# Single-head scores in the even block, transposed retention queries and keys, and a new order of the first loads in a three-block fp32 transformer kernel

## The chip, the cores and the metric

The kernel runs on one core of a Trainium2 chip. The metric is the device time in microseconds (us) from launch to end. The engines are TensorE (PE, matrix products; PEld are its weight loads), VectorE (DVE), ScalarE (ACT), GpSimd (POOL) and SyncE (SP, which here only issues DMA transfers).

## The reference

Batch 1, 256 tokens, width 1024, everything in fp32. Three blocks follow one another, and a last rmsnorm ends the program.

```
# block 0 (even): two kinds of attention, then an MLP
h = rmsnorm(x, g);  qa, ka, va, qb, kb, vb = split(h @ w_in_e)
qa, ka, qb, kb = rmsnorm per head of 64
oa = window attention: 8 query heads over 2 kv heads, ALiBi slopes, a sink per head
ob = neighbourhood attention: 8 heads, relative position bias
x = x + concat(oa, ob) @ w_out_e;  x = x + relu(rmsnorm(x) @ w1)**2 @ w2
# block 1 (odd): retention, then an MLP
q, k, v, g = split(rmsnorm(x) @ w_in_o)      # 8 heads, dk = 128, dv = 256
y = forward retention + backward retention (decays per head)
x = x + (silu(g) * groupnorm(y)) @ w_out_o;  x = x + MLP(x)
# block 2: moba + indexed sparse + cross attention, gated and merged
z = rmsnorm(x) @ w_in;  u = sum of three gated branches;  x = x + u @ w_out
return rmsnorm(x, g_final)
```

## The kernel before

All weights stream from memory in chunks of 1 MB (the first two in quarters) into four `raw` buffers, in the order in which they are used: `load` and `w_dma` issue them on SP's queue, each chunk when its buffer is free. ACT copies a chunk to `whi` in a rounded format (fp32r), DVE makes the rest `wlo = raw - whi`, half a chunk at a time. Activations are split in the same way (`xh`, `xl`). Each product is three matmuls, high by high, high by low and low by high (`mm3`), so a name such as `whi,xh` in a row is moving operand, stationary operand. `panel` computes 512 columns of a product for the 256 tokens with x as the stationary operand and the weights moving: 8 blocks of the width by 2 token tiles by 3, 48 matmuls of 512 columns (one of 256 columns wide takes 48 of 256). `panel_T` holds the weights and moves x, 256 tokens at a time, so its result lies transposed, features by tokens; for the same 512 columns it takes 96 matmuls of 256 columns.

Fp32 matmuls without a split are the attention scores (`kTa,qTa` for the window heads, `kTb,qTb` for the neighbourhood heads) and the PE transposes (`const,qn`, `const,p`, `const,nat`, `const,at`). A score is a product over 64 features. The heads of a pair lie in rows 0 to 63 and 64 to 127 of the array, and `score_pair` writes their matmuls alternately, for each of two token tiles one matmul of each head, into two banks. `even_head` follows for each head: a DVE pass adds the bias table and finds the maximum, ACT takes the exponential, DVE normalises, PE transposes p (`const,p`), ACT and DVE split it (`ph`, `pl`), and PE multiplies by v.

A scheduler inside the build writes one order for each engine. Tasks are generators. Each operation asks for an engine, has a cost in a table and becomes ready when its inputs are (by the same costs); of the ready operations the one with the lowest priority number goes first. `MEM`, `BIAS` and `DMA0` are times in the scheduler's own clock from which mem, the bias tables and the first transfers count, and `pads()` and `distances()` are low-priority tasks that start at a time of that clock. The order that comes out is fixed in the program; on the chip each engine follows it and waits where an input is late.

Start-up: `warm()` fills PE with bf16 matmuls of zeros until the third half-chunk of weights is split. The first panel (qa) runs from chunks 0 and 1, the second (ka with va, 256 columns, here called the ka panel) from chunks 2 and 3, and then qb, kb and vb. In the odd block, for each of four pairs of heads (hp), a `panel` computes q and k of both heads, ACT copies the result to `nat`, PE transposes it in two groups of four, and ACT and DVE split it into `qk`; then come a panel for v and one for the gate.

Of the kernel before, what the change touches and what calls it, by code (L numbers as in the profile page):

```python
# [72 lines left out]
class Kernel:  # L73
# [17 lines left out]
    MEM, BIAS = 14.0, 16.0  # L91

    DMA0, FINE = 1.5, 4
# [299 lines left out]
    def load(self, eng, out, in_):  # L393

        eng.dma_start(out, in_)
        n = out.shape[0] * self._n(out) * 4
        self.free["D"] += max(n / 360e3, 0.18)
        self._mark(self.ready, out, self.free["D"] + 1.7, "D")

    def w_dma(self, a=None, b=4):  # L400
# [13 lines left out]
        else:  # L414
            self.nc.sync.dma_start(raw[:, :n], src)
            t0 = max(self.free["D"], self.rawfree[i - self.RAW] if i >= self.RAW else 0.0)
            self.free["D"] = t0 + P * n * 4 / 360e3
# [259 lines left out]
    def split_T(self, src, hi, lo, k0, t, key, scale=None):  # L677
# [8 lines left out]
        if k0 is None:  # L686
            pv = ps[:, :n * P].rearrange("p (a b q) -> p a b q", a=2, b=n // 2)
        else:
            pv = ps[:, :n * P].rearrange("p (i q) -> p i q", i=n)
            hi, lo = (v[:, k0:k0 + n, t * P:(t + 1) * P] for v in (hi, lo))  # L690
# [46 lines left out]
    def even_head(self, pool, ps, v, o, j, tab, init, sink=None):  # L737


# [102 lines left out]
    def run(self):  # L842
# [24 lines left out]
        self.w_dma(0, 4)  # L867
        for t in range(NT):
            self.load(nc.sync, x[t], aps["x"][t * P:(t + 1) * P, :])
        self.load(nc.sync, const, aps["const"][:, :K_MAIN])  # L870
        for _ in range(self.RAW - 2):
            self.w_dma()
# [9 lines left out]
    def warm(self):  # L882
# [6 lines left out]
        yield 1.4  # L889
        while self.hcur < 3:  # L890
# [4 lines left out]
            self._pe(0.213 if self.now < 7 else 0.11, ps)  # L895
# [36 lines left out]
    def _even(self, pool):  # L932
# [62 lines left out]
        self.spawn(pads(), 12.0, self.LOW)  # L995
# [16 lines left out]
        self.spawn(distances(), 20.0, self.LOW)  # L1012
# [15 lines left out]
        def even_heads():  # L1028

            self.res["hd"] = self.hb  # L1030
            for j in range(0, 16, 2):
# [4 lines left out]
                if j % 4 == 0:  # L1036
# [3 lines left out]
                qT, kT = (qTa, kTa[:, 0, :]) if j < 8 else (qTb, kTb[:, j // 2 - 4, :])  # L1040
                rows = [slice(0, 64), slice(64, P)]
                ps = yield from self.score_pair([[(t * S, (t + 1) * S, qT[r, j // 2 % 4, t * P:(t + 1) * P], kT[r])
                                                  for r in rows] for t in range(NT)])
                self.fire(("s", j), ("s", j + 1))
                for i in range(2):
                    yield ("acq", "hd", 1)
                    self.spawn(head_a(j + i, o, ps[i]) if j < 8 else head_b(j + i - 8, o, ps[i]))
# [34 lines left out]
        def head_a(j, o, ps):  # L1082
            h, n = A_ORDER[j], j % 2
            vc = slice(64 * n, 64 * n + P)
# [4 lines left out]
            return self.even_head(pool, ps, lambda kt: (va[kt][0][:, vc], va[kt][1][:, vc]), o, j, tab,  # L1089
# [7 lines left out]
        def head_b(h, o, ps):  # L1097
# [4 lines left out]
            return self.even_head(pool, ps, lambda kt: (vb[kt][0][:, vc], vb[kt][1][:, vc]), o, 8 + h, tab, 3e38)  # L1102
# [127 lines left out]
    def _odd(self, pool):  # L1230
# [32 lines left out]
        def qk_task(hp, qk):  # L1263
            def task(t, ps):
                yield ("acq", "nat", 1)
                nat = pool.tile([P, 512], F32, name="nat", tag="nat", bufs=2)
                yield from self.act(nat, ps, AF.Copy)
                self.done(ps)
                yield from self.split_T(nat, *(vap(v[:, t * P:], [[KO, 2], [S, 2], [1, P]]) for v in qk), None, t,
                                        ("rqk", hp, t))  # L1270
                self.give("nat")
            return task
# [100 lines left out]
        for hp in range(4):  # L1373
# [5 lines left out]
            yield from self.panel(self.xT, "xo", qk_task(hp, qk), tmajor=hp == 0)  # L1379
            for hh in range(2):  # L1380
                self.spawn(head(hp, hh, qk, vv, sg), hh * 4.0)
            yield from self.panel(self.xT, "xo", v_task(hp, vv))
# [375 lines left out]
def _layout(inputs):  # L1758
# [32 lines left out]
    for hp in range(4):  # L1791
        parts += [w[:, hp * 256:(hp + 1) * 256], w[:, D + hp * 256:D + (hp + 1) * 256],
                  w[:, 2 * D + hp * 512:2 * D + (hp + 1) * 512], w[:, 4 * D + hp * 512:4 * D + (hp + 1) * 512]]
# [38 lines left out]
```

## Time and profile before

| what | value |
| --- | --- |
| median of 3 runs | 996.02 us (996.0, 996.02 and 997.14) |
| profiled execution | 997.11 us, its span 995.3 us |
| PE busy | 982.2 us, 99% of the span |
| DVE, ACT, POOL busy | 675.1, 525.9 and 30.4 us |
| granted clock, mean | 0.997 of full speed |
| DMA | 175.71 MB, 177 GB/s on average |

The span runs from the first to the last instruction of the profile; 1.8 us of the execution lie outside it. Busy time of PE is time with at least one matmul under way. Because matmuls are pipelined, a matmul's own duration is longer than the step from one start to the next, and the step is what a matmul costs in a stream.

### The profile page before, as it was taken

The page shows a single profiled execution, that of the slowest core. Times are in us where ns is not written, and L with a number is a line of the kernel's source. Part 1 is how long each engine was busy: PE and PEld are TensorE (multiplying, and loading weights), DVE is VectorE, ACT ScalarE, POOL GpSimd, SP SyncE. Part 2 cuts the span into 40 slices and gives each one's busy share as a digit, 9 for nine tenths or more (in the row PEclk, how much of TensorE's full clock was granted, in tenths as well). Part 3 has the DMA queues.
Part 4 walks back from the last instruction along what each step waited for, and adds up shares of the span by engine and source line. Part 5 has one row for each costly group of instructions (what it writes and reads, how often), then busy time and mean ns, then how long its engine had stood idle before and what let it go on. Part 6 is the DMA issues. An engine that isn't in the chain of part 4 may idle for free.

```text
span 995.3 us, 14096 instructions
## 1 busy us (share of the span) xinstructions
PE 982.2 (99%) x5559; PEld 844.6 (85%) x5559; DVE 675.1 (68%) x1134; ACT 525.9 (53%) x821; POOL 30.4 (3%) x38
## 2 busy tenths in 40 slices
PE   8999999999999999999999999999999999999997
PEld 6787889999998888888889999998888888878885
DVE  6898567554457977877657555446779866677774
ACT  7777656433345655555446553334564554454453
POOL 1220000000000000000000000000100000000000
PEclk9999999999999999999999999999999999999999
DMA  9733455555445544443555555542544436544431
GB/s 351 285 133 122 134 175 205 218 209 202 170 169 175 184 166 163 167 168 138 194 187 171 209 209 214 212 171 97 203 157 141 156 139 205 192 173 148 180 127 42
DMA packets 27266, 175.71 MB, mean 177 GB/s; under 512 B 3200, under 2 KB 3584, under 8 KB 7616
## 3 DMA queue, kind: packets, MB, share of 16 engines
q1 hardware_dynamic: 25776, 171.49, 48.0%
q0 software_dynamic: 704, 2.49, 1.0%
q8 instruction: 43, 0.70, 0.3%
q10 hardware_dynamic: 720, 0.84, 0.3%
q14 instruction: 23, 0.19, 0.1%
HBM read 173.75 MB, written 1.05 MB: 176 GB/s over the span
## 4 chain that ended last, share of the span: by engine, by line
PE 97%; DVE 2%; ACT 0%; DMA 0%; issue 0%; POOL 0%; DVEq 0%; POOLq 0%
PE bank L332 93%; PE bank L343 4%; DVE p L279 1%; DMA tb<-in_xT 0%; DVE pl L257 0%; DVE p L265 0%; DVE st L289 0%; PE bank L894 0%; ACT ph L252 0%; ACT nraw L252 0%; ACT u L252 0%; DVE x L257 0%; DVE wlo L257 0%; ACT qn L252 0%; DVE o L257 0%
## 5 line engine op out<-in xcount | busy, mean ns | idle before, releaser
L257 DVE TENSOR_TENSOR wlo<-raw,whi 128x1024 fp32r<-128x1024 f32 (+2 forms) x266 | 311.5, 1183 | 89.6 <-ACT whi L252 87.9
L252 ACT ACTIVATE whi<-raw 128x1024 fp32r<-128x1024 f32 (+2 forms) x266 | 268.5, 1024 | 131.9 <-PE bank L332 131.3
L332 PE MATMUL bank<-whi,xh 128*128 128x512 f32 (+2 forms) x592 | 233.8, 397 | 2.2 <-ACT whi L252 2.2
L332 PE MATMUL bank<-wlo,xh 128*128 128x512 f32 (+2 forms) x592 | 227.5, 384 | 0.4 <-DVE wlo L257 0.4
L332 PE MATMUL bank<-whi,xl 128*128 128x512 f32 (+2 forms) x592 | 227.7, 385 | 0.0
L332 PEld LDWEIGHTS bank<-whi,xh 128*128 128x128 f32 x592 | 112.2, 190 | 23.0 <-ACT whi L252 3.1
L332 PEld LDWEIGHTS bank<-whi,xl 128*128 128x128 f32 x592 | 112.2, 190 | 22.2
L332 PEld LDWEIGHTS bank<-wlo,xh 128*128 128x128 f32 x592 | 112.5, 190 | 19.7 <-DVE wlo L257 0.6
L332 PE MATMUL bank<-xh,mlo 128*128 128x256 f32 x464 | 128.2, 276 | 0.0
L332 PE MATMUL bank<-xh,mhi 128*128 128x256 f32 x464 | 128.2, 276 | 0.0
L332 PE MATMUL bank<-xl,mhi 128*128 128x256 f32 x464 | 128.2, 276 | 0.0
L257 DVE TENSOR_TENSOR h<-h 128x512 f32<-128x512 f32 x32 | 22.0, 688 | 115.4 <-ACT h L252 115.4
L332 PE MATMUL bank<-whi,hh 128*128 128x512 f32 x256 | 100.2, 391 | 0.0
L332 PE MATMUL bank<-wlo,hh 128*128 128x512 f32 x256 | 99.8, 390 | 0.0
L332 PE MATMUL bank<-whi,hl 128*128 128x512 f32 x256 | 99.7, 389 | 0.0
L252 ACT ACTIVATE h<-bank 128x512 f32<-128x512 f32 x32 | 18.8, 588 | 137.4 <-PE bank L332 137.4
L332 PEld LDWEIGHTS bank<-xh,mhi 128*128 128x128 f32 x464 | 87.1, 188 | 0.5
L332 PEld LDWEIGHTS bank<-xl,mhi 128*128 128x128 f32 x464 | 87.1, 188 | 0.4
L332 PEld LDWEIGHTS bank<-xh,mlo 128*128 128x128 f32 x464 | 87.1, 188 | 0.0
L257 DVE TENSOR_TENSOR mlo<-raw,mhi 128x1024 fp32r<-128x1024 f32 x58 | 68.6, 1219 | 1.2 <-ACT mhi L252 1.2
L252 ACT ACTIVATE mhi<-raw 128x1024 fp32r<-128x1024 f32 x58 | 58.2, 1047 | 0.8 <-PE bank L332 0.8
L332 PEld LDWEIGHTS bank<-whi,hl 128*128 128x128 f32 x256 | 48.1, 188 | 10.2
(250 smaller groups left out, 1337.3 us busy)
## 6 DMA issues: line engine op xcount, KB each, us to landing
raw<-in_w_mlp_in SPq DMA_DIRECT2D x32, 1024.0 KB, 4.9
raw<-in_w_mlp_out SPq DMA_DIRECT2D x32, 1024.0 KB, 4.9
raw<-in_w_in SPq DMA_DIRECT2D x32, 1024.0 KB, 4.8
raw<-in_w_in_o SPq DMA_DIRECT2D x24, 1024.0 KB, 4.8
raw<-in_w_out_o SPq DMA_DIRECT2D x8, 1024.0 KB, 4.9
raw<-in_w_in_e SPq DMA_DIRECT2D x6, 1024.0 KB, 9.2
raw<-in_w_up SPq DMA_DIRECT2D x6, 1024.0 KB, 4.7
raw<-in_w_mem SPq DMA_DIRECT2D x4, 1024.0 KB, 4.9
```

The source lines that it names most:

```text
L252: self.nc.scalar.activation(out, in_, func, scale=scale, **kw)
L257: self.nc.vector.tensor_tensor(out, a, b, op=op)
L279: self.nc.vector.tensor_tensor_reduce(out, a, b, scale, init, op0, op1, acc)
L332: self.nc.tensor.matmul(out, lhsT, rhs, start=start, stop=stop, skip_group_check=shared)
L343: self.nc.tensor.transpose(out, in_, self.ident)
```

## The change

Five things change.

1. The even block's 16 heads no longer share `score_pair`. Each head takes one bank and issues its own two matmuls. The last block still pairs its scores.
2. In the odd block q and k come from `panel_T` and are split from PSUM directly; `nat`, its copy and its transposes go, and so does `split_T`'s case for them. For hp 0 the v panel now comes ahead of q and k. The host packs `w_in_o` to match.
3. `warm()` issues 24 matmuls of zeros without a condition before it looks at the weights.
4. The transfers of chunks 2 and 3 are issued ahead of x and the constants.
5. Numbers of the scheduler: `BIAS` 16 to 30, `DMA0` 1.5 to 2.3, the rate of the transfers 360e3 to 405e3, `pads()` 12 to 20, `distances()` 20 to 28. They change the order only.

```
@@ -88,9 +88,9 @@
-    MEM, BIAS = 14.0, 16.0
-    DMA0, FINE = 1.5, 4
+    MEM, BIAS = 14.0, 30.0
+    DMA0, WARM, FINE = 2.3, 24, 4
@@ -394,7 +394,7 @@
         n = out.shape[0] * self._n(out) * 4
-        self.free["D"] += max(n / 360e3, 0.18)
+        self.free["D"] += max(n / 405e3, 0.18)
         self._mark(self.ready, out, self.free["D"] + 1.7, "D")
@@ -414,7 +414,7 @@
             t0 = max(self.free["D"], self.rawfree[i - self.RAW] if i >= self.RAW else 0.0)
-            self.free["D"] = t0 + P * n * 4 / 360e3
+            self.free["D"] = t0 + P * n * 4 / 405e3
             self._mark(self.ready, raw, self.free["D"] + 2.2, "D")
@@ -683,11 +683,8 @@
             self.transpose(ps[:, i * P:(i + 1) * P], src[:, i * P:(i + 1) * P])
-        if k0 is None:
-            pv = ps[:, :n * P].rearrange("p (a b q) -> p a b q", a=2, b=n // 2)
-        else:
-            pv = ps[:, :n * P].rearrange("p (i q) -> p i q", i=n)
-            hi, lo = (v[:, k0:k0 + n, t * P:(t + 1) * P] for v in (hi, lo))
+        pv = ps[:, :n * P].rearrange("p (i q) -> p i q", i=n)
+        hi, lo = (v[:, k0:k0 + n, t * P:(t + 1) * P] for v in (hi, lo))
         end = yield from self.split(hi, lo, pv, scale)
@@ -734,9 +731,14 @@
-    def even_head(self, pool, ps, v, o, j, tab, init, sink=None):
+    def even_head(self, pool, q, kT, v, o, j, tab, init, sink=None):
+        yield ("acq", "bank", 1)
+        ps = self.bank()
+        yield ("op", "T", [], [])
+        for t in range(NT):
+            self.mm(ps[:, t * S:(t + 1) * S], q(t), kT, True, True)
+        self.fire(("s", j))
         p = pool.tile([P, 512], F32, name="p", tag="p", bufs=self.hb)
@@ -865,11 +867,11 @@
         self.w_dma(0, 4)
+        for _ in range(self.RAW - 2):
+            self.w_dma()
         for t in range(NT):
         self.load(nc.sync, const, aps["const"][:, :K_MAIN])
-        for _ in range(self.RAW - 2):
-            self.w_dma()
         self.mhalf = self.mt([P, 16], "mhalf")
@@ -887,12 +889,15 @@
         yield 1.4
+        for _ in range(self.WARM):
+            self.nc.tensor.matmul(ps[:, :256], zero[:, :P], zero[:, :256], start=True, stop=True)
+            self._pe(0.213, ps)
         while self.hcur < 3:
             self.nc.tensor.matmul(ps[:, :256], zero[:, :P], zero[:, :256], start=True, stop=True)
-            self._pe(0.213 if self.now < 7 else 0.11, ps)
+            self._pe(0.11, ps)
         self.done(ps)
@@ -992,7 +997,7 @@
                 yield from self.act(vap(v[:, 64:], [[192, n], [1, 64]]), vap(self.const[:, K_CM:], [[0, n], [1, 64]]), AF.Copy)
-        self.spawn(pads(), 12.0, self.LOW)
+        self.spawn(pads(), 20.0, self.LOW)
         qTb = pool.tile([P, 4, S], F32, name="qTb", tag="qTb")
@@ -1009,7 +1014,7 @@
                 self.fire(("tab", j))
-        self.spawn(distances(), 20.0, self.LOW)
+        self.spawn(distances(), 28.0, self.LOW)
@@ -1028,7 +1033,7 @@
             self.res["hd"] = self.hb
-            for j in range(0, 16, 2):
+            for j in range(16):
                 if j == 0:
@@ -1037,14 +1042,8 @@
                     self.spawn(out_group(j // 4, o))
-                qT, kT = (qTa, kTa[:, 0, :]) if j < 8 else (qTb, kTb[:, j // 2 - 4, :])
-                rows = [slice(0, 64), slice(64, P)]
-                ps = yield from self.score_pair([[(t * S, (t + 1) * S, qT[r, j // 2 % 4, t * P:(t + 1) * P], kT[r])
-                                                  for r in rows] for t in range(NT)])
-                self.fire(("s", j), ("s", j + 1))
-                for i in range(2):
-                    yield ("acq", "hd", 1)
-                    self.spawn(head_a(j + i, o, ps[i]) if j < 8 else head_b(j + i - 8, o, ps[i]))
+                yield ("acq", "hd", 1)
+                self.spawn(head_a(j, o) if j < 8 else head_b(j - 8, o))
@@ -1079,14 +1078,15 @@
-        def head_a(j, o, ps):
+        def head_a(j, o):
             h, n = A_ORDER[j], j % 2
-            vc = slice(64 * n, 64 * n + P)
+            rows, vc = slice(64 * n, 64 * n + 64), slice(64 * n, 64 * n + P)
                 return tabs.pop(j)
-            return self.even_head(pool, ps, lambda kt: (va[kt][0][:, vc], va[kt][1][:, vc]), o, j, tab,
+            return self.even_head(pool, lambda t: qTa[rows, j // 2, t * P:(t + 1) * P], kTa[rows, 0, :],
+                                  lambda kt: (va[kt][0][:, vc], va[kt][1][:, vc]), o, j, tab,
                                   nsink[:, h:h + 1], cols[:, C_SINK + h:C_SINK + h + 1])
@@ -1094,12 +1094,15 @@
-        def head_b(h, o, ps):
+        def head_b(h, o):
+            rows = slice(64 * (h % 2), 64 * (h % 2) + 64)
             vc = slice(h // 2 * 192 + h % 2 * 64, h // 2 * 192 + h % 2 * 64 + P)
-            return self.even_head(pool, ps, lambda kt: (vb[kt][0][:, vc], vb[kt][1][:, vc]), o, 8 + h, tab, 3e38)
+            return self.even_head(pool, lambda t: qTb[rows, h // 2, t * P:(t + 1) * P], kTb[rows, h // 2, :],
+                                  lambda kt: (vb[kt][0][:, vc], vb[kt][1][:, vc]), o, 8 + h, tab, 3e38)
         def vb_task(t, ps):
@@ -1261,14 +1264,11 @@
         def qk_task(hp, qk):
-            def task(t, ps):
-                yield ("acq", "nat", 1)
-                nat = pool.tile([P, 512], F32, name="nat", tag="nat", bufs=2)
-                yield from self.act(nat, ps, AF.Copy)
+            def task(b, ps):
+                qs = slice(b * KO, b * KO + 2 * S)
+                end = yield from self.split(qk[0][:, qs], qk[1][:, qs], ps)
                 self.done(ps)
-                yield from self.split_T(nat, *(vap(v[:, t * P:], [[KO, 2], [S, 2], [1, P]]) for v in qk), None, t,
-                                        ("rqk", hp, t))
-                self.give("nat")
+                self.fire(("rqk", hp, b), at=end)
             return task
@@ -1376,10 +1376,13 @@
             sg = [pool.tile([P, 512], F32, name=f"sg{t}", tag=f"sg{t}", bufs=2) for t in range(NT)]
-            yield from self.panel(self.xT, "xo", qk_task(hp, qk), tmajor=hp == 0)
+            if hp == 0:
+                yield from self.panel(self.xT, "xo", v_task(hp, vv), tmajor=True)
+            yield from self.panel_T(self.xT, "xo", qk_task(hp, qk))
             for hh in range(2):
                 self.spawn(head(hp, hh, qk, vv, sg), hh * 4.0)
-            yield from self.panel(self.xT, "xo", v_task(hp, vv))
+            if hp > 0:
+                yield from self.panel(self.xT, "xo", v_task(hp, vv))
             yield from self.panel(self.xT, "xo", g_task(hp, sg))
@@ -1789,8 +1792,9 @@
     for hp in range(4):
-        parts += [w[:, hp * 256:(hp + 1) * 256], w[:, D + hp * 256:D + (hp + 1) * 256],
-                  w[:, 2 * D + hp * 512:2 * D + (hp + 1) * 512], w[:, 4 * D + hp * 512:4 * D + (hp + 1) * 512]]
+        qk = [w[:, hp * 256:(hp + 1) * 256], w[:, D + hp * 256:D + (hp + 1) * 256]]
+        v = [w[:, 2 * D + hp * 512:2 * D + (hp + 1) * 512]]
+        parts += (v + qk if hp == 0 else qk + v) + [w[:, 4 * D + hp * 512:4 * D + (hp + 1) * 512]]
     f["w_in_o"] = _pack(np.concatenate(parts, 1), _uniform(6 * D))
     for l in range(2):
```

Counted over the whole program, PE issues 32 transposes fewer; 192 panel matmuls of 512 columns become 384 of 256 columns; ACT issues 8 copies of 512 columns fewer. The number of score matmuls, 16 heads by two, stays.

The order on ACT at the start, before. `nraw<-x` are squares for the rmsnorm, `vah`, `val` and `vbh` fill constant columns, `qn<-bank` squares the first panel's result, and the two rows `whi<-raw` behind them are chunk 2 and chunk 3 of the weights.

```order
L252 ACTIVATE whi<-raw 128x512
L252 ACTIVATE nraw,ss_112<-x_70 128x512 x2
L252 ACTIVATE nraw,ss_113<-x_71 128x512 x2
L252 ACTIVATE vah_121<-const 128x64
L252 ACTIVATE val_122<-const 128x64
L252 ACTIVATE vah_123<-const 128x64
L252 ACTIVATE qn<-bank 128x512
L252 ACTIVATE val_124<-const 128x64
L252 ACTIVATE qn<-bank 128x512
L252 ACTIVATE vbh_127<-const 128x4x64
L252 ACTIVATE whi<-raw 128x512 x2
L252 ACTIVATE vbl_128<-const 128x4x64
```

The same place now:

```order
L252 ACTIVATE whi<-raw 128x512 x3
L252 ACTIVATE nraw,ss_112<-x_70 128x512
L252 ACTIVATE whi<-raw 128x512
L252 ACTIVATE nraw,ss_112<-x_70 128x512
L252 ACTIVATE nraw,ss_113<-x_71 128x512 x2
L252 ACTIVATE qn<-bank 128x512 x2
L252 ACTIVATE vah_121<-const 128x64
L252 ACTIVATE val_122<-const 128x64
L252 ACTIVATE vah_123<-const 128x64
L252 ACTIVATE val_124<-const 128x64
L252 ACTIVATE vbh_127<-const 128x4x64
L252 ACTIVATE whi<-raw 128x1024 x2
```

All four halves of chunks 2 and 3 now stand ahead of the squares of the first panel, and the constant columns behind them.

The order on PE where the window heads' scores begin, before. Banks 516 and 517 are the two heads of the first pair, 522 and 523 those of the second.

```order
L332 MATMUL bank_516<-kTa_120,qTa_119 128x256
L332 MATMUL bank_517<-kTa_120,qTa_119 128x256
L332 MATMUL bank_516<-kTa_120,qTa_119 128x256
L332 MATMUL bank_517<-kTa_120,qTa_119 128x256
L332 MATMUL bank_522<-kTa_120,qTa_119 128x256
L332 MATMUL bank_523<-kTa_120,qTa_119 128x256
L332 MATMUL bank_522<-kTa_120,qTa_119 128x256
L332 MATMUL bank_523<-kTa_120,qTa_119 128x256
L332 MATMUL bank_411<-whi_413,xh_114 128x512
```

The same place now; each bank is one head, the first in rows 0 to 63, the next in rows 64 to 127, and so on.

```order
L332 MATMUL bank_545<-kTa_120,qTa_119 128x256 x2
L332 MATMUL bank_546<-kTa_120,qTa_119 128x256 x2
L332 MATMUL bank_560<-kTa_120,qTa_119 128x256 x2
L343 MATMUL bank_572<-const_72,qn_505 128x128 x4
L332 MATMUL bank_518<-whi_418,xh_114 128x512
L332 MATMUL bank_518<-wlo_440,xh_114 128x512
L332 MATMUL bank_518<-whi_418,xl_115 128x512
L332 MATMUL bank_589<-kTa_120,qTa_119 128x256 x2
L343 MATMUL bank_600<-const_72,qn_537 128x128 x4
```

Before, the scores stand in six groups without other work between their matmuls, of 4, 2, 2 heads (window) and 4, 2, 2 heads (neighbourhood). Now they stand in nine, of 3, 1, 2, 1, 1 and 4, 1, 2, 1 heads, and within a group both matmuls of one head come ahead of those of the next.

The order on PE where q and k of the first pair of retention heads are computed, before:

```order
L332 MATMUL bank<-whi,xl 128x512
L343 MATMUL bank<-const,nat 128x128 x4
L332 MATMUL bank<-whi,xh 128x512
L332 MATMUL bank<-wlo,xh 128x512
L332 MATMUL bank<-whi,xl 128x512
```

The same panel now:

```order
L332 MATMUL bank<-xh,whi 128x256
L332 MATMUL bank<-xl,whi 128x256
L332 MATMUL bank<-xh,wlo 128x256
L332 MATMUL bank<-xh,whi 128x256
L332 MATMUL bank<-xl,whi 128x256
```

There were eight such groups of transposes in the block, two for each pair of heads; now there is none, and x moves through stationary weights.

## Rows read from the trace of the kernel before

**Rows 1.** The page, part 4: shares of the chain that ended last, by engine.

```profile
PE 97%; DVE 2%; ACT 0%; DMA 0%; issue 0%; POOL 0%; DVEq 0%; POOLq 0%
```

**Rows 2.** PE's waits: line, what it waited for, us, times, longest.

```profile
PE bank L332 <- DVE pl L257: 1.4, 4, 0.6
PE bank L332 <- ACT ph L252: 1.3, 3, 0.7
```

**Rows 3.** Timeline of PE from the start: start, us, engine, line, operands, count, [idle before].

```profile
1.09 4.24 PE L894 MATMUL bank<-vx 128*128 128x256 bf16 x19 [1.09 <-DVE vx L885]
5.88 1.22 PE L332 MATMUL bank<-whi,xh 128*128 128x512 f32 x2 [0.55 <-ACT whi L252]
...
19.52 0.39 PE L332 MATMUL bank<-whi,xl 128*128 128x512 f32 x1
21.60 0.38 PE L332 MATMUL bank<-whi,xh 128*128 128x256 f32 x1 [1.69 <-ACT whi L252]
...
30.45 0.40 PE L332 MATMUL bank<-whi,xh 128*128 128x512 f32 x1
```

**Rows 4.** Timeline of ACT, 15 to 24 us.

```profile
15.75 0.63 ACT L252 ACTIVATE nraw<-x 128x512 f32<-128x512 f32 x1
...
19.50 0.60 ACT L252 ACTIVATE qn<-bank 128x512 f32<-128x512 f32 x1 [1.97 <-PE bank L332]
...
20.92 1.15 ACT L252 ACTIVATE whi<-raw 128x512 fp32r<-128x512 f32 x2
```

**Rows 5.** Timeline of SP's queue, the start: issues of x and of chunks 2, 3.

```profile
8.59 0.91 SPq L395 DMA_DIRECT2D x<-in_x  x2
...
10.65 1.02 SPq L415 DMA_DIRECT2D raw<-in_w_in_e  x2
```

**Rows 6.** Windows: stretch, us, busy PE (x), PEld, DVE, ACT, POOL, PEclk, DMA, GB/s.

```profile
23.50:26.91 3.41, 3.41 (x19) 3.41 (x17) 2.74 (x6) 2.42 (x4) 2.39 (x2) 0.52 1.04 437
```

**Rows 7.** Timeline of PE in the odd block, around one group of transposes.

```profile
327.63 0.39 PE L332 MATMUL bank<-whi,xl 128*128 128x512 f32 x1
...
329.22 0.60 PE L343 MATMUL bank<-const,nat 128*128 128x128 f32 x4
329.58 0.48 PE L332 MATMUL bank<-whi,xh 128*128 128x512 f32 x1
329.89 0.40 PE L332 MATMUL bank<-wlo,xh 128*128 128x512 f32 x1
```

**Rows 8.** Timeline of PE in block 0's MLP, 256-column matmuls with stationary weights.

```profile
147.10 0.28 PE L332 MATMUL bank<-xh,whi 128*128 128x256 f32 x1
...
151.06 0.28 PE L332 MATMUL bank<-xh,whi 128*128 128x256 f32 x1
```

**Rows 9.** Timeline of PE, the first scores.

```profile
40.14 0.40 PE L332 MATMUL bank<-whi,xl 128*128 128x512 f32 x1
40.47 2.00 PE L332 MATMUL bank<-kTa,qTa 64*128 64x256 f32 x16
42.40 0.51 PE L332 MATMUL bank<-whi,xh 128*128 128x512 f32 x1
42.74 0.39 PE L332 MATMUL bank<-wlo,xh 128*128 128x512 f32 x1
...
43.96 1.13 PE L332 MATMUL bank<-kTa,qTa 64*128 64x256 f32 x8
```

**Rows 10.** The same timeline cut at 40.60 us: records that began by then.

```profile
40.47 0.49 PE L332 MATMUL bank<-kTa,qTa 64*128 64x256 f32 x2
```

**Rows 11.** Timeline of DVE: first bias pass and normalisation of a head, twice.

```profile
41.63 0.48 DVE L279 CUSTOM_DVE_ANT_0 p<-bank,tab,nsink 128x256 f32<-128x256 f32 x1 [0.95 <-PE bank L332]
...
44.53 0.60 DVE L265 TENSOR_SCALAR p<-p,den 128x256 f32<-128x256 f32 x2
...
86.03 0.42 DVE L279 CUSTOM_DVE_ANT_0 p<-bank,tb 128x256 f32<-128x256 f32 x1
...
88.15 0.61 DVE L265 TENSOR_SCALAR p<-p,den 128x256 f32<-128x256 f32 x2
```

## The prediction

> **What bounds the kernel now.** I read the page first, for the chain that ended last, then PE's waits, then the timelines of the stretches that the diff touches. The chain is 97% PE [rows 1], and PE is busy for 982.2 of the 995.3 us of the span, so time can only come from three places: a stretch in which PE waits, a stretch in which its matmuls run at a slow clock, and matmuls that need not be there. PE's idle time is 13.1 us in all. In the heads of the even block 2.7 us of it are waits for `ph` and `pl`, the two halves of a transposed p [rows 2]. At the start PE stands for 0.55 us ahead of the first real matmul and for 1.69 us between the first panel and the ka panel [rows 3]. The rest of the start, and what follows the last matmul, the change leaves as it is. The MLPs and the whole last block issue the same matmuls in the same order as before; I cost them at nothing, and their cover is that same order.
>
> **The start.** Before, PE ends the first panel with the matmul that starts at 19.52, one step of 0.23 later, at 19.75. The ka panel starts at 21.60 [rows 3]. What it waits for is `whi` of chunk 2, and ACT made that at 20.92, behind the squares `qn<-bank`, which themselves wait for the first panel's end at 19.50 [rows 4]. So PE waits for ACT, which waited for PE. Then the ka panel runs from 21.60 to 30.45, 8.85 us [rows 3]. It holds two groups of four transposes at 0.44 (below), and its 48 matmuls at the step of 0.120 that 256 columns take (151.06 less 147.10 is 33 steps [rows 8]) would be 5.76; 2.2 us are left over. They lie mostly in the stretch 23.50 to 26.91, where the granted clock is 0.52, half of full speed [rows 6], so the lower of the two levels, 1.2 GHz; that fall follows the two stretches in which PE stood.
>
> Now ACT makes all of `whi` for the ka panel ahead of the squares. SP issued x at 8.59 and chunks 2 and 3 at 10.65 [rows 5]; the second half of x was in use by ACT at 15.75 [rows 4], so the chunks, which take x's place in the queue, should be there by about that time. ACT needs 0.575 for each of four halves (1.15 for two [rows 4]) and DVE about as much, beside other work: the last `wlo` by about 18.8. The first panel starts later: 24 matmuls of zeros at 4.24 / 19 = 0.223 us are 5.4, from 1.09 to about 6.4 instead of 5.88 [rows 3]. But its end is set by its weights, not its start: its last quarter chunks come when they came, and they let PE end between 17.5 and 19.75. I take 18.5, because 24 unbroken matmuls leave no gap of 0.55 behind which PE could stay at the slow step of 0.223 for 256 columns that it shows up to there. The ka panel then ends at about 24.4, when its 5.76 us follow without a stall, and no fall of the clock comes, since PE hasn't stood. Against 30.45, less 0.88 for the two groups of transposes, which now stand in the qb panel, that is 5.2 less. If the first panel ends at 19.75 as before, it is 4.1; if neither data nor clock hold it up, 5.6. Late next is the first half of the chunk behind, which the qb panel wants at 24.4 and which by the pace of the transfers is split at about that time; what it may lack is in the upper end. x and the constants are about 2.5 us later; the first thing on PE that needs the rmsnorm's factor is P times v, some 20 us later, so I cost that at nothing. The constant columns of v behind the squares are hidden by the same 20 us, and the bias tables, which are late next, by the 10 us from the ka panel to the scores. **-5.2 (-4.1 to -5.6).**
>
> **Retention.** A group of four `nat` transposes puts the second matmul behind it 0.67 us after its own start, where one matmul's step accounts for 0.227 [rows 7]: 0.44 us for each of eight groups, 3.5 us removed. 192 matmuls of 512 columns at 0.227 (1.59 for seven steps, 327.63 to 329.22 [rows 7]) are 43.6 us; the 384 of 256 columns in their place are 46.1 at 0.120 [rows 8], 2.5 more. ACT's copies go, but ACT isn't late there. For hp 0 the v panel now stands ahead of q and k, so what lies between v and its use grows and what lies between the gate's panel and the rest shrinks; 5.7 us of panel remain ahead of the transposes of `at`, which I take as enough. The step behind a group may be long once more, which would make it -1.3, and a step of 0.1205 makes it -0.8. **-1.0 (-1.3 to -0.8).**
>
> **The scores.** Here the change adds time. Each 64-row score is two records. The group of 16 records takes 2.00 us and that of 8 takes 1.13 [rows 9]; half the records are 0.87, so 8 records are four slots of 0.2155 with two records in each, one of each head. The timeline cut at 40.60 shows two records begun by then [rows 10], so the heads of a pair do run side by side. What a group costs beyond its slots: it starts 0.10 later than a step after the matmul at 40.14, lasts 0.21 beyond eight slots (40.47 to 42.40), and the step behind it is 0.34 instead of 0.23 [rows 9], together 0.41. Six groups and 32 slots are 9.4 us.
>
> Now there are nine groups, 3.7 us of such ends. If the scores of one head run beside those of the next wherever two heads stand next to each other, the slots are 8 + 4 + 4 + 4 + 4 for the groups of 3, 1, 2, 1, 1 heads and 8 + 4 + 4 + 4 for those of 4, 1, 2, 1: 44, or 9.5 us. The sum is 13.2, 3.8 more than before. If only the second matmul of a head overlaps with the next head's first, it is 50 slots and 5.1 more. No row shows two matmuls of one row group followed by two of the other, so both ends stay; I take 4.2, since records do start in twos although each matmul is two records and program order alone would put them behind one another. **+4.2 (+3.8 to +5.1).** Where eight transposes of p or of `at` stood together, four and four stand apart now: eight more switches in the two blocks. The step behind a group, 0.31 where 0.23 is usual (329.58 to 329.89 [rows 7]), is the most that one can cost, 0.08: **+0.3 (0 to 0.6)**.
>
> The Trainium skill, "TensorE: Matmul & The Clock Gate", Part 3, under "What overlaps and what doesn't", says that matmuls start and end strictly in program order. Rows 10 speak against the strict reading for two records, and no run here yet shows it for whole heads; by the rule the single heads would lie behind one another, which is the first rival below.
>
> **The waits of the heads.** The 2.7 us of waits for `ph` and `pl` [rows 2] come where P times v follows the transposes of the same head with at most four to eight transposes between. Now every head has at least 1.8 us of panel, scores or another head's work there. What may appear is a wait ahead of the transposes. The chain from a head's first bias pass to the end of its normalisation takes 3.5 us (41.63 to 45.13) and 2.7 (86.03 to 88.76) [rows 11]. In the new order the first neighbourhood head has some 2.6 us between its scores and its transposes (the other three heads' scores and six panel matmuls), the others 4 and more. That leaves about 0.5 to 1.1 us of wait in place of 2.7. **-1.7 (-2.7 to +1.0)**; the upper end is the old waits staying and one head in each group late by its full 0.9 us.
>
> **Sum.** On the profile's own 997.11: -5.2 - 1.0 + 4.2 + 0.3 - 1.7 = -3.4, so 993.7. The profile is 1.1 above the median of the runs, 996.02, and one of the three runs is as high as it. If the fall of the clock in the ka panel is what the higher ones have, then both come down to the same number, since the change takes that fall away; so I hold to 993.7, 2.3 below the median. 0.2% is 2.0 us here, about what a measurement can tell: below 994.0 is faster, above 998.0 slower.
>
> **Rivals.**
> 1. *Heads in sequence.* Neighbouring single heads don't overlap: 57 slots if only joints overlap, 64 if nothing does, so +6.6 to +8.1 in place of +4.2. 996.1 to 997.6, no change to be measured. For it: nothing in the new order puts the other row group's matmul next. Against it: rows 10. 0.15.
> 2. *The softmax chain comes to light (slower).* In pairs, two heads' scores went to PE together, far ahead. Single heads start later, and if DVE, which is also the one that makes `wlo`, takes each head's bias pass half a microsecond later than the order assumes, PE stands ahead of each head's transposes. From 0.28 us for each of 16 heads on it decides (998.0 less 993.7); at 0.5 it is 8 us, and 1001.7. For it: PE waits exactly on this chain now. Against it: all heads but the first of the neighbourhood group have 4 us of cover for a chain of 3.5. 0.10.
> 3. *The start gives less.* Chunks 2 and 3 come later than x did, or the clock stays low in the first panel, and the ka panel ends at 26 instead of 24.4; 995.3, no change. For it: all 16 DMA engines are busy in that stretch, and the start of the first panel moves back. 0.08.
> 4. *More than forecast*: no waits at all in the heads, and the start at its lower end, 992.0 and less. 0.05.
>
> **How the numbers follow.** The forecast's case has 0.62: its own range is 992.0 to 995.7, and three quarters of it lie below 994.0. Faster: 0.47 + 0.05 = 0.52. Same: 0.15 + 0.15 + 0.08 = 0.38. Slower: 0.10. The range reaches down to 991.5, the sum of the low ends of the start and the waits, and up to 997.4, which takes in nearly all of the first rival and leaves out the second: 0.15 or so.
>
> **What would show it.** On PE's timeline: the ka panel starts without idle time ahead of it and ends near 24.4, and no window after 9.85 shows a granted clock of 0.52. In the scores: groups of 6, 2, 4, 2 and 2 matmuls (twice as many records); one head alone takes 4 slots, so 0.86 and its ends; a pair of heads that takes as long as one shows the overlap, one that takes 1.7 shows the first rival. PE's waits for `ph` and `pl` are all but gone, and those for `p` are no more than 1.1 us in all; several for `p` would be the second rival. In the odd block no gap and a step of 0.120 in the new panels; a step of 0.125 or more would cost 2 us. The forecast is wrong above all if the single heads are slower than 5 us, or if the ka panel still waits.

## The result and the profile after

The changed kernel takes 990.34 us (median of 4 runs, 990.0 to 990.78) against 996.01 before: a ratio of 0.9941, interval 0.9924 to 0.9958. On another chip it was 990.44 and 0.9937 (0.9923 to 0.9951; x11 below). The forecast was 993.7, and 991.5 at the least: the way was right, and the gain was larger. Of the eleven runs of x4 below, one took 1407.57 us at a granted clock of 0.654 and stands outside its ratio.

The profiled execution takes 990.0 us, 7.1 less than that of before, of which 1.1 is that execution's distance from its median. The windows below cut both kernels at the same events: end of the ka panel, first matmul of the even block's output product, first matmul of the odd block behind its last rmsnorm transposes, first matmul of the retention's output product. The second window is called the heads' stretch from here on; it begins with the qb panel. Columns as in [rows 6]. Before:

```profile
0.00:30.45 30.45, 26.74 (x131) 21.36 (x132) 18.64 (x42) 20.48 (x45) 5.54 (x8) 0.94 0.93 364
30.45:121.36 90.91, 87.98 (x492) 71.38 (x491) 73.38 (x203) 65.71 (x152) 11.10 (x8) 1.00 0.43 157
121.36:322.99 201.63, 201.63 (x1288) 182.05 (x1286) 119.38 (x133) 98.15 (x125) 0.72 (x1) 1.00 0.53 188
322.99:476.08 153.09, 153.09 (x773) 129.68 (x771) 118.85 (x232) 89.32 (x124) 6.72 (x10) 1.00 0.48 167
476.08:995.30 519.22, 512.72 (x2883) 440.19 (x2881) 344.87 (x527) 252.25 (x377) 6.36 (x11) 1.00 0.47 167
```

The changed kernel:

```profile
0.00:24.26 24.26, 22.22 (x123) 18.04 (x124) 15.55 (x37) 18.23 (x40) 4.02 (x8) 1.00 0.92 345
24.26:115.32 91.06, 90.88 (x500) 73.96 (x499) 76.79 (x210) 67.73 (x158) 12.71 (x9) 1.00 0.49 186
115.32:316.94 201.62, 201.62 (x1287) 182.04 (x1286) 119.36 (x133) 98.15 (x125) 0.72 (x1) 1.00 0.52 188
316.94:468.69 151.75, 151.75 (x934) 136.69 (x932) 119.10 (x232) 84.99 (x116) 7.64 (x10) 1.00 0.48 169
468.69:988.20 519.51, 512.68 (x2883) 440.16 (x2881) 344.72 (x527) 252.24 (x377) 6.37 (x11) 1.00 0.47 167
```

The start gives 6.2 us, of which about 0.9 are the eight transposes that now stand in the next window. That window is as long as before, 91.06 for 90.91, though it holds these and single scores: less the 0.9, it is 0.7 shorter, where the forecast had it 2.8 longer. The retention gives 1.34; the first MLP is equal. The last window is 0.3 longer, all of it behind the last matmul (6.8 us for 6.5), which the forecast left as it was; why stays open.

PE's waits, the view of [rows 2], which leaves out waits under 0.15 us, have two rows left; those for `ph`, `pl` and p are gone:

```profile
PE bank L893 <- DVE vx L887: 1.1, 1, 1.1
PE bank L332 <- ACT whi L252: 0.9, 2, 0.7
```

The start on PE, which answers to [rows 3] (timeline):

```profile
1.09 4.72 PE L893 MATMUL bank<-vx 128*128 128x256 bf16 x24 [1.09 <-DVE vx L887]
6.08 0.74 PE L332 MATMUL bank<-whi,xh 128*128 128x512 f32 x2 [0.27 <-ACT whi L252]
7.49 0.73 PE L332 MATMUL bank<-whi,xh 128*128 128x512 f32 x2 [0.67 <-ACT whi L252]
8.06 0.40 PE L332 MATMUL bank<-wlo,xh 128*128 128x512 f32 x1
8.30 0.39 PE L332 MATMUL bank<-whi,xl 128*128 128x512 f32 x1
...
18.28 0.39 PE L332 MATMUL bank<-whi,xl 128*128 128x512 f32 x1
18.51 0.28 PE L332 MATMUL bank<-whi,xh 128*128 128x256 f32 x1
...
24.26 0.40 PE L332 MATMUL bank<-whi,xh 128*128 128x512 f32 x1
```

The ka panel follows the first without idle time and runs in 5.75 us. The loop of 24 does not close the gap ahead of the first real matmul, which was 0.55 us before [rows 3]: PE stands for 0.27 and then for 0.67 us. But the loop's last matmuls already step by 0.11 us for 256 columns, where its first ones step by 0.21, and at 8.06 the matmuls of 512 columns step by 0.24, full pace. In the kernel before, at the same time, they stepped by 0.43, the pace of the lower level. This is read from the steps alone, since the view's granted clock is 1.00 for all of the first 10 us in both kernels (timeline of PE, before):

```profile
8.41 0.63 PE L332 MATMUL bank<-wlo,xh 128*128 128x512 f32 x1
8.84 0.63 PE L332 MATMUL bank<-whi,xl 128*128 128x512 f32 x1
```

On ACT, `whi` of chunks 2 and 3 comes between 14.4 and 18.2, ahead of the squares of the first panel (`qn<-bank`), which answers to [rows 4]:

```profile
15.76 0.63 ACT L252 ACTIVATE whi<-raw 128x512 fp32r<-128x512 f32 x1 [0.21 <-DVE wlo L257]
...
17.53 0.62 ACT L252 ACTIVATE whi<-raw 128x512 fp32r<-128x512 f32 x1
...
19.89 1.06 ACT L252 ACTIVATE qn<-bank 128x512 f32<-128x512 f32 x2
```

The single scores, which answer to [rows 9]: three heads, one head, and (50.12) two heads.

```profile
38.57 1.99 PE L332 MATMUL bank<-kTa,qTa 64*128 64x256 f32 x12
40.49 0.66 PE L343 MATMUL bank<-const,qn 128*128 128x128 f32 x4
...
41.77 1.13 PE L332 MATMUL bank<-kTa,qTa 64*128 64x256 f32 x4
...
50.12 1.14 PE L332 MATMUL bank<-kTa,qTa 64*128 64x256 f32 x8
51.19 0.66 PE L343 MATMUL bank<-const,p 128*128 128x128 f32 x4
```

One head takes 1.13 us, and two take 1.14: the second runs wholly beside the first. Three take 1.99, about as four do (2.00 in pairs before [rows 9], 2.10 here at 82.36). So the slots are the 44 of the full overlap, and the first rival is out. The Trainium skill, "TensorE: Matmul & The Clock Gate", Part 3, "What overlaps and what doesn't", has matmuls start and end strictly in program order. This trace decides against it for whole heads: both matmuls of the second head stand behind both of the first in program order, and yet they don't lengthen the group. From the start of each of the nine groups to the next matmul the scores take 11.51 us, for 8.11 in the six before: 3.4 more.

Ahead of the transposes of p one short wait is left, that of the first neighbourhood head: the matmul ahead runs out at 86.04, and the transposes start 0.12 later.

```profile
85.65 0.39 PE L332 MATMUL bank<-whi,ml 128*128 128x512 f32 x1
86.17 0.81 PE L343 MATMUL bank<-const,p 128*128 128x128 f32 x4
```

The new q and k panel in the odd block (timeline of PE) takes 96 steps of 0.120, 11.52 us, where 48 of 512 columns and two groups of transposes stood:

```profile
326.57 0.28 PE L332 MATMUL bank<-xh,whi 128*128 128x256 f32 x1
...
338.09 0.40 PE L332 MATMUL bank<-whi,xh 128*128 128x512 f32 x1
```

### The profile page after: what moved, and what is told of

It is laid out like the page before. It is cut to its first block, busy times and chain, and to the rows that moved or that the text cites. A ratio compares the mean times of both kernels' runs of the same rounds, so it can differ in the third digit from the quotient of the medians.

```text
span 988.2 us, 14418 instructions
## 1 busy us (share of the span) xinstructions
PE 979.2 (99%) x5719; PEld 850.9 (86%) x5719; DVE 675.5 (68%) x1134; ACT 521.3 (53%) x813; POOL 31.5 (3%) x38
## 4 chain that ended last, share of the span: by engine, by line
PE 98%; DMA 1%; DVE 0%; ACT 0%; issue 0%; POOLq 0%; ACTq 0%
PE bank L332 94%; PE bank L343 4%; DMA tb<-in_xT 1%; DVE wlo L257 0%; ACT nraw L252 0%; ACT u L252 0%; DVE x L257 0%; DVE p L279 0%; POOLq L1822 0%; ACT whi L252 0%; ACT xh L252 0%; ACTq L395 0%; PE bank L899 0%; DVE p L265 0%; DVE r L273 0%
## 5 line engine op out<-in xcount | busy, mean ns | idle before, releaser
L332 PE MATMUL bank<-whi,xh 128*128 128x512 f32 (+2 forms) x528 | 206.5, 393 | 0.9 <-ACT whi L252 0.9
L332 PE MATMUL bank<-whi,xl 128*128 128x512 f32 (+2 forms) x528 | 201.6, 382 | 0.0
L332 PE MATMUL bank<-wlo,xh 128*128 128x512 f32 (+2 forms) x528 | 201.3, 381 | 0.0
L332 PEld LDWEIGHTS bank<-whi,xl 128*128 128x128 f32 x528 | 99.2, 188 | 19.5
L332 PEld LDWEIGHTS bank<-whi,xh 128*128 128x128 f32 x528 | 99.1, 188 | 19.1 <-ACT whi L252 1.7
L332 PEld LDWEIGHTS bank<-wlo,xh 128*128 128x128 f32 x528 | 99.5, 188 | 16.5
```

What stands on the lines that cost most here:

```text
L332: self.nc.tensor.matmul(out, lhsT, rhs, start=start, stop=stop, skip_group_check=shared)
```

## The experiments

Each ratio is to the kernel before on the same chip, with its 95% interval.

| run | median us | ratio (interval) |
| --- | --- | --- |
| x1 all pairs | 992.58 | 0.9959 (0.9946 to 0.9973) |
| x2 old retention | 992.63 | 0.9959 (0.9946 to 0.9971) |
| x3 single heads alone | 995.82 | 0.9994 (0.9985 to 1.0003) |
| x4 before again | 996.85 | 1.0002 (0.9993 to 1.0011) |
| x5 warm-up alone | 995.61 | 0.9997 (0.9988 to 1.0006) |
| x6 order of loads alone | 994.28 | 0.9974 (0.9965 to 0.9982) |
| x7 old numbers | 991.87 | 0.9958 (0.9946 to 0.9971) |
| x8 slow split | 1003.37 | 1.0074 (1.006 to 1.0087) |
| x9 neighbourhood pairs | 988.96 | 0.9928 (0.9916 to 0.9941) |
| x10 conditional warm-up | 990.29 | 0.9943 (0.9929 to 0.9956) |
| x11 changed again | 990.44 | 0.9937 (0.9923 to 0.9951) |
| x12 neighbourhood pairs again | 988.62 | 0.9919 (0.9905 to 0.9932) |

**x1, all heads in pairs.** The changed kernel, with part 1 of the change undone:

```
-            for j in range(16):
+            for j in range(0, 16, 2):
...
+                ps = yield from self.score_pair(...)
```

> The changed kernel with the even block's heads in pairs again; everything else as changed. Theory A (single heads are not what pays: their scores cost 3.4 us more and the waits of the heads go away with the new order of the rest): the scores take 8.1 us again, PE waits 1 to 2 us in the neighbourhood heads, the median falls to about 989. Theory B (single heads are what takes the waits away): the scores give back 3.4, but idle time of about 2.7 us and what hangs on it, together 4.7, comes back, median 991 to 992.

It is 2.2 us above the changed kernel: the way theory B had it, beyond its 992, and by more than the waits. Timeline and windows of PE in this run:

```profile
75.98 2.86 PE L332 MATMUL bank<-kTb,qTb 64*128 64x256 f32 x24
80.69 0.72 PE L343 MATMUL bank<-const,p 128*128 128x128 f32 x4 [1.85 <-DVE p L265]
```

```profile
82.00:85.00 3.00, 2.67 (x11) 1.98 (x11) 3.00 (x11) 1.94 (x6) 0.00 (x0) 0.50 0.00 0
85.00:88.00 3.00, 3.00 (x16) 3.00 (x15) 2.41 (x11) 1.57 (x5) 0.00 (x0) 0.50 0.00 0
```

Six heads' scores stand in a row with nothing behind them but their own transposes; PE waits 1.85 us for the first p, and then the granted clock is 0.50 for the whole of 82 to 88, the lower level. There the products P times v run at half pace; all of them together take 15.6 us, for 11.9 in the changed kernel. The scores without that wait are 8.2 us. Pairing is cheaper on PE; the order that it leads to here isn't.

**x2, old retention.** The changed kernel with part 2 undone (`panel`, `nat`, `split_T` back).

> The changed kernel with the retention of before (x stationary, nat, transposes). If the retention's part is worth what the two traces show between the end of the first MLP and the start of the retention's output product, 1.34 us, the median is 991.5 to 991.9 and the rest of the trace is unmoved. If the gain there is given back or comes from something else, the median stays at 990.3.

From its first matmul in the odd block (317.36) to the retention's output product (470.45) it takes 153.09 us, to the hundredth that of before: the part is worth 1.34 us. The median is 2.3 up, 1.0 above what was expected; in the profile 0.44 of that lies in the heads' stretch, whose order is the same, behind a wait of 0.23 for `qn` at 34.5. In x11 such a wait is 0.38, with the heads' stretch at 91.61 and a median of 990.44. So the size of what is left over is not settled.

**x3, single heads alone.** The kernel before with part 1 only.

> The kernel before with head-by-head scores alone: the order on PE stays the same in all else, groups of 4, 2, 2 and 4, 2, 2 heads, but in each group both matmuls of a head stand ahead of those of the next. If neighbouring heads run side by side (theory A), the scores take 8.1 to 8.5 us and the time stays within 0.5 us of the kernel before. If program order holds them back (theory B), they take 10.5 to 15 us and the median rises by 2.4 to 7 us, to 998 or more.

The expectation was wrong on the order: the scheduler places single heads apart under the old numbers too, in groups of 4, 1, 1, 1, 1 and 4, 1, 2, 1. So its total of 11.5 us for the scores is no test of overlap. Its first group is one: the 4 heads at 39.90 take 2.03 us from start to next start, and a group of two pairs takes 1.93 [rows 9]. What the run does show: with scores of 11.5 us PE is idle in the heads' stretch for 0.6 us instead of 2.9, the stretch is 90.59 for 90.91, and no change is measured. Here single heads pay for themselves by the waits that go with their order.

**x4, before again.** No edit.

> The kernel before, profiled once more. Its runs lie at 995.8 to 996.0 or at 997.1. Theory A: the higher ones have the stretch of granted clock 0.52 in the ka panel or a longer one, the lower ones less of it; a profile of a lower run then shows the ka panel ending about 1 us earlier than 30.45. Theory B: the difference lies elsewhere, and the ka panel ends at 30.4 in a run of 996.0 too.

The profiled run took 997.33 us, and its ka panel ends at 30.71; no low run was profiled. From there to the last matmul it takes 957.9 us, as the profile of before does (988.41 less 30.45): the two differ ahead of that point alone. Over the four profiles with the old order of loads (x5, x3, before and x4) the ka panel ends at 28.69, 29.88, 30.45 and 30.71, and the runs take 995.43, 996.52, 997.11 and 997.33 us. This points to the start for the spread of 995 to 998; two of the four are other kernels, so it is not shown.

**x5 and x6, the two parts of the start, each alone in the kernel before.** x5 is the loop of 24 matmuls; x6 moves the loads and takes the scheduler's new numbers for transfers (`DMA0`, and the rate of 405e3, whose lines are left out here):

```
+        for _ in range(self.RAW - 2):
+            self.w_dma()
         for t in range(NT):
...
+    DMA0, FINE = 2.3, 4
```

> The kernel before with the 24 unconditional matmuls of zeros alone; chunks 2 and 3 still come behind x, and their high parts still stand behind the squares on ACT. Theory A (the gap of 0.55 us ahead of the first real matmul keeps the clock low until 9.85): without it matmuls run at full pace by 8 us, the first panel ends at 18.3 to 18.8 instead of 19.75, the ka panel still waits 1.7 us and still meets the lower clock; gain about 1 us. Theory B (the weights set the end of the first panel): no change.

> The kernel before with the transfers of chunks 2 and 3 ahead of x and the scheduler's numbers for transfers, and with the conditional warm-up of before. Theory A (the ka panel waits because its high parts stand behind the squares on ACT, and the low clock follows from that wait): no idle time ahead of the ka panel, no granted clock near 0.5 in 18 to 27 us, ka panel done by 25.5, that is 4 us of the 5.3. Theory B (the unbroken warm-up is needed for it): the clock falls again and the ka panel ends at 27 or later. What the heads do in their new order (pairs) comes on top: -1 to +1.

The start of the ka panel in x5 (timeline of PE):

```profile
19.86 0.38 PE L332 MATMUL bank<-whi,xh 128*128 128x256 f32 x1 [1.54 <-ACT whi L252]
20.60 0.43 PE L332 MATMUL bank<-wlo,xh 128*128 128x256 f32 x1 [0.35 <-DVE wlo L257]
```

Windows of x5 and, second, of x6:

```profile
21.00:24.00 3.00, 3.00 (x16) 3.00 (x15) 2.62 (x7) 3.00 (x6) 2.99 (x2) 0.50 1.02 425
```

```profile
21.00:24.00 3.00, 3.00 (x27) 3.00 (x27) 2.26 (x5) 2.86 (x6) 3.00 (x2) 1.00 0.99 411
```

In x5 PE ends the first panel at 18.2, where it was 19.75 before, then stands for 1.54 and 0.35 us ahead of and in the ka panel, meets the clock of 0.50, and ends it at 28.69. In the trace that is theory A, and the profile is 1.7 us shorter than the one of before; the median over eleven runs does not show it. In x6 there is no idle time ahead of the ka panel and no fall of the clock, and the ka panel ends at 24.06, theory A again. But x6 is not the order alone: with the new numbers the scheduler puts 22 matmuls of zeros ahead of the first real one instead of 19, and the first panel ends as early as in x5. What the order of the loads and of ACT gives by itself is the step from x5 to x6: 4.6 us, less 0.9 for the eight transposes that leave the ka panel, of a gain of 5.3 in all. The profiled run of x6, 992.09, is the lowest of eleven. In it the heads, in pairs, wait, 1.6 us for `qn` and 2.0 for `ph` and `pl`, and their stretch is 92.34. Why the other runs of x6 take up to 995.28, so that its median gains only 2 us, no trace shows.

**x10, the changed kernel with the conditional warm-up** (part 3 undone).

> The changed kernel with the conditional warm-up of before (22 matmuls of zeros, two real ones, two more of zeros, and so on, as the scheduler's clock has it). Theory A (the 24 unbroken matmuls add to the start): the ka panel ends 0.3 to 1 us later than 24.26, or the runs spread over 2 us and more as those with the new order of loads and the old warm-up did (992.1 to 995.3), median 990.8 to 992. Theory B (the order of loads is all of it): ka panel done at 24.1 to 24.3, median 990.0 to 990.6.

Theory B in the median. The 22 matmuls that the new numbers put ahead of the first real one reach up to it without a gap, here as in x6. The ka panel ends at 24.52, between the two theories, in a profile of the highest of the five runs (991.34).

**x7, old numbers.** The changed kernel with BIAS 16, `pads()` 12, `distances()` 20.

> The changed kernel with BIAS 16, pads 12 and distances 20 as before: single heads, the new start and the new retention. Theory A (the single heads by themselves keep the waits away): PE's waits in the heads stay under 0.8 us and the median within 0.7 of 990.3. Theory B (the later bias tables make the room): waits of 2 us and more in the heads, median 992 or more.

PE's waits:

```profile
PE bank L343 <- DVE qn L257: 1.9, 2, 1.2
PE bank L343 <- DVE p L265: 0.2, 1, 0.2
```

Neither theory: the waits for `ph`, `pl` and p are gone without the later bias tables, but two others appear ahead of the scores, for `qn`, the normalised q and k. The median is 1.5 above the changed kernel. The numbers are worth that much, at a place that the forecast had costed at nothing. The heads' stretch grows by 2.03 us for 1.97 more of idle time; the order on PE differs from that of the changed kernel from 33.4 us on, so this does not measure what a wait costs.

**x8, a slow split.** The order on PE is unchanged; two more copies are put ahead of the split of each p, so work is added:

```
+        for _ in range(2):
+            self.nc.scalar.activation(ph, ps, AF.Copy)
         yield from self.split(ph, pl, ps)
```

> The changed kernel with the high part of each transposed p copied three times on ACT, so that it and the low part come 1.1 us later; the order on PE is that of the changed kernel. Work is added, no result changes. It makes PE wait for them in some of the 16 heads. Theory A (a wait costs PE its idle time and 0.2 to 0.3 us more, because the matmuls ahead run out and the next ones start anew): the heads' stretch grows by the idle time plus 0.25 for each wait. Theory B (a wait costs its idle time): it grows by the idle time alone.

The heads' stretch as a window, to be read beside 24.26 to 115.32 above:

```profile
24.24:128.48 104.24, 96.78 (x500) 74.58 (x499) 77.88 (x209) 85.67 (x188) 11.99 (x9) 1.00 0.42 162
```

It is 13.2 us longer. PE's idle time in it is 7.46 (104.24 less 96.78) for 0.18: 7.3 more, in 24 rows with idle time of over 0.02 us for 2. The other 5.9 us are in PE's busy time, at a clock of 1.00 and with the same 500 matmuls: 0.27 for each of the 22 new waits. Nearly all of the 13.2 lies in the steps at these waits and right behind them. Theory A. The 0.27 is a mean: the two waits right behind scores add only 0.07 each. x2, x10 and x11 have the order of the changed kernel in this stretch too, with one wait more: 0.23, 0.74 and 0.38 us more of idle time lengthen it by 0.44, 1.10 and 0.55.

**x9 and x12, pairs for the neighbourhood heads only, with x11 beside x12.**

```
+                if j >= 8:
+                    if j % 2 == 0:
...
+                        pair = yield from self.score_pair(...)
```

> The changed kernel with pairs for the eight neighbourhood heads alone; the window heads stay single, and the order up to the first neighbourhood score is the changed kernel's, so that panel matmuls of the memory product still stand between scores and transposes. Theory A (what costs the pairs their time in the run with all heads paired is the wait of 1.85 us and the clock behind it, not pairing): the neighbourhood scores take 4.1 us instead of 5.2, no wait above 0.6 us and no granted clock of 0.5, heads' stretch 0.3 to 1.1 us shorter, median 989.2 to 990.2. Theory B (pairs bring waits wherever they stand): 1 us and more of waits for p, ph or pl in these heads, median 991 or more.

> The changed kernel once more, on the same chip as the next. Theory A (its low spread is its own): 990.0 to 990.8 again, ka panel done at 24.0 to 24.5. Theory B (the runs differ by chip and by the half chunk behind the ka panel, which comes in time or 0.75 us late): a spread of 1 us and more, and up to 991.4.

> The changed kernel with pairs for the neighbourhood heads, beside the changed kernel on one chip. If its gain is that of the scores (1.16 us) and no wait comes back, its median lies 0.9 to 1.4 below that of the changed kernel; if the lower time before was that chip's, the two are within 0.5.

Timeline of PE in x9, the neighbourhood scores:

```profile
83.28 2.00 PE L332 MATMUL bank<-kTb,qTb 64*128 64x256 f32 x16
87.50 1.14 PE L332 MATMUL bank<-kTb,qTb 64*128 64x256 f32 x8
94.69 1.14 PE L332 MATMUL bank<-kTb,qTb 64*128 64x256 f32 x8
```

Two groups of one head are gone, the scores of the block take 10.35 instead of 11.51, and no wait of the heads themselves is above 0.06. On one chip it is 988.62 (988.33 to 989.06) against 990.44 (990.24 to 990.57): 1.8 us, more than the scores' 1.2; it is the fastest version here. The transposes and P times v take 0.7 less as well from start to next start (21.4 us in x12, 22.1 in x11), for a reason that stays open. The run shows that x1's loss is not in pairing, but in what stands between the scores and the transposes. Its one new wait, 0.75 us for `wlo` in the qb panel, is the late half chunk that the forecast named; the profiles of x10 and x12 have it too, those of the changed kernel don't.

```profile
25.34 0.50 PE L332 MATMUL bank<-wlo,xh 128*128 128x512 f32 x1 [0.75 <-DVE wlo L257]
```

## Why the prediction was wrong

- **The start, -5.2 forecast.** 6.2 less 0.9 for the transposes is 5.3. The ka panel starts at 18.51 and ends at 24.26, for 18.5 and 24.4 in the forecast. The wait and the clock behind it went as forecast, by the order (x5 against x6). The reason given for 18.5 was wrong in part, and the number was luck to that extent: the 24 matmuls left gaps of 0.27 and 0.67 us, and the full pace was reached ahead of them. The 22 conditional ones of x10 do as well, so the loop itself adds nothing that the medians show.
- **Retention, -1.0.** It is 1.34, in the windows and in x2, with the four split groups of `at` in it, for which half of the +0.3 stood.
- **The scores, +4.2.** They cost 3.4 from start to next start, and by [rows 9] 0.2 for entering and leaving each of three more groups, which lies in the steps around them: 4.0. The full overlap, 44 slots, was the right case.
- **The waits of the heads, -1.7 (-2.7 at most). This step failed.** All of PE's idle time in the heads went (2.9 to 0.2), since no wait ahead of the transposes of p came but one of 0.12, where 0.5 to 1.1 was expected. And its worth was mis-sized: from start to next start, the transposes and P times v took 26.1 us before and 22.1 after, with eight more transposes (0.7) among these: 4.7 less, where the idle time is 2.7 less. A wait costs more than its idle time. Before, at one of them (timeline of PE, before):

```profile
48.15 0.28 PE L332 MATMUL bank<-ph,val 128*128 128x256 f32 x1
48.66 0.39 PE L332 MATMUL bank<-pl,vah 128*128 128x256 f32 x1 [0.23 <-DVE pl L257]
48.88 0.28 PE L332 MATMUL bank<-ph,vah 128*128 128x256 f32 x1
49.00 0.28 PE L332 MATMUL bank<-ph,val 128*128 128x256 f32 x1
```

The steps are 0.51 and 0.22 where 0.12 is usual: 0.50 lost for 0.23 of idle time. The matmul ahead counts as busy until it has run out (0.28, an end that the profile models), and the one behind starts anew. So the idle time of the table is less than what a wait costs. The eight waits make 2.0 in this way (4.7 less 2.7); by x8's 0.27 each it would be 2.2. So the lower end of that term, all idle time gone, was no bound.
- **The sum.** -5.3, -0.7 in the heads, -1.3 and +0.3 at the end make -7.0 for the measured 7.1. Of the 3.6 to 3.7 between -3.4 and these, the waits make 3.0. The base, the profile's own 997.11, fits: 997.1 less 7.1 is where the changed kernel's runs lie. Its reason, that the higher runs of the kernel before have the fall of the clock, the four profiles named under x4 make likely and do not show. The low end of the range is mis-added: 993.7 less the 0.4 and 1.0 by which the start and the waits could be lower is 992.3 and not 991.5.
- **The rivals.** Heads in sequence: refuted. The softmax chain: not in this order; but x1 is that mechanism, in pairs, with 1.85 us and the clock behind it. The start gives less: refuted, the ka panel ends at 24.26 and not at 26. More than forecast, which had 0.05: this is what came, without its lower start; the waits of the heads are gone, but it priced their going at 1.0 beyond the forecast, and it was 3.0. The change of numbers, costed at nothing, is worth 1.5 (x7), by the waits for `qn` that the old ones bring.

## What to carry to other kernels

A wait in the middle of a stream of short matmuls is to be priced at its idle time plus the run-out of the matmul ahead and the new start of the one behind, here 0.27 us; several short waits are worth more than their sum in the table of waits. A matmul arrangement that is cheaper by itself can lose if it bunches work: what lies between a producer and its consumer decides. Pairing only where other work follows gives both, cheap scores and no wait (x9). When the end of one panel and the input of the next wait for each other through a third engine's order, moving that engine's rows is worth the wait and the clock behind it.

## What the runs showed of the hardware that was not expected

Two fp32 products of 64 rows in different halves of the rows ran side by side although two matmuls of the first (four records) stood ahead of the second's: 1.14 us for two heads, 1.13 for one. A wait of 1.85 us on PE was followed by a granted clock of 0.50 for about 6 us (x1), and waits of up to 1.1 us, 7.5 us of them in 104, by none (x8).
